# A hybrid encoder step: SSD states handed over with the state index on partitions, final states in 512-column products, scan in runs of four heads

## The chip, the cores and the metric

The kernel runs on one core of one Trainium2 chip. The metric is device microseconds of one execution; lower is better. TensorE (PE in the profile) multiplies matrices, VectorE (DVE), ScalarE (ACT) and GpSimd (POOL) work element by element, and SyncE (SP) issues most of the transfers between memory and the on-chip buffers. An fp32 product that the program writes as one matmul appears as two instructions on PE in the trace.

## The reference

One layer of an encoder works on two groups of tokens that share the weights: 256 tokens of a new stream (the prompt) and the next 32 tokens of a running stream (the sample). Of it, the part that matters here is the SSD mixer: 32 heads of 64 channels in two groups of 16, each head with a state of 64 x 128 numbers. `xs` holds the convolved inputs, `dt` the step sizes, `B` and `C` the projections shared by a group's heads, `a = dt * A` the log decays, and `h0` the old state (zero for the prompt):

```
states = einsum('bclgn,bcgjl,bclgjp->bcgjpn', Bc, decay_states, xc)   # xc = xs * dt
h_last, h_prev = scan: h -> chunk_decay * h + states                  # starts from h0
y = diag part (C B^T, masked and decayed, times xc) + (C h_prev exp(acum)) + D * xs
```

The layer goes on with the gate and a grouped norm, multiplies the concatenation of pooling mixer and SSD mixer with `w_out` (3072 x 2048), adds the input after a norm, and ends in a convolved FFN (2048 -> 2 x 5632 -> 2048). Outputs are the tokens and all new states, among them `h_last` of the prompt and of the sample (32 x 64 x 128 each).

## The kernel before, in words

Activations lie transposed: channels on partitions, 288 tokens (256 + 32) on the free axis. Each weight matrix goes through `project` (L172): blocks of 8 x 128 rows by 256 columns (1 MB) are fetched by SP, split into a high part `whi` on ScalarE (L151) and a low part `wlo` on VectorE (L152), and each 128 x 128 block is multiplied three times (L168 to L170) with the split activations: 288 columns per instruction. The buffers for raw, high and low parts are four deep. Nearly all of TensorE's work is this.

In what order each engine runs its instructions is decided at build time by a scheduler from the program's order, its own estimate of durations, and priorities (a fetch and a split of weights may go ahead); at run time each engine works through its list in that order and waits for what isn't ready. Products land in eight PSUM banks, five for `project` and the state products, three (`aux`) for all else.

The stages around the change:

- B, C and dt columns of `w_in` come first. From dt, `g` holds the running sums of decays of each head over 416 columns (256 for the first 128 source tokens, 128 for the next, 32 for the sample), written to memory as `g_d`. `tok` and `tokd` hold, per token on partitions, the sums, dt, and dt times the decay to the end (`dec`), transposed by TensorE in blocks of 128, 128 and 32 tokens (L464 to L471). `cbt` holds the masked products of B and C (L492 to L501), the sample's as a 32 x 32 block.
- The x columns of `w_in` follow in eight projections of two 128-channel tiles. Each tile is convolved (`conv_out`, L389) and written token by token to memory as `xs_d`.
- The scan of two heads (one 128-channel tile) is `ssd_pair` (L527). `XS_RATE` and `Z_RATE` say after which of the eight x and eight z projections how many pairs are recorded. For every four heads `ssd_four` (L510) loads `g_d` broadcast to all partitions (`gb`) and the old state `h0`, and transposes the state with two products on TensorE (L518) and a ScalarE copy (L520). A pair loads its `xs_d` columns (`xk`), weighs them by dt (`xw`, L540, in two instructions for 128 and 32 rows), makes the decay tables `m` with six Relus (L549), one exponential (L552) and a product with `cbt` (L553), and then multiplies: two prompt blocks (L559, L561), the sample block on 32 rows (L563) and the old state (L565), each for two heads, which sit on the two halves of TensorE's columns. L566 adds D times xs and gives the tile.
- After the scan: gating and norm sums, the u columns of `w_in` with the pooling mixer (`pool_tile`, `pool_group`, L720 to L753), then `w_out` in seven groups of columns (L848). A state step sits between these groups: `state_in` (L805) loads a tile's `xs_d` columns and old state through POOL's queue, and VectorE weighs them (L816 to L819). `state_mm` (L822) multiplies them with B: three products of 128 columns with `xw` stationary and B moving, for two prompt blocks and the sample (32 rows). ScalarE copies the two results out (L832), POOL adds the decayed old state (L833), and SP stores both (L834, L835). Twelve tiles are done three at a time behind four groups; four are kept for the moment when the norm behind `w_out` is computed: one before and three behind `spread` (L585), which sends the norm's factors to all partitions (L864 to L868).
- Then VectorE and ScalarE make the FFN's input tiles `hn` one by one (L872 to L893), and the FFN projections start on them.

Of the kernel before, what the change touches and what calls it, by code (L numbers as in the profile page):

```python
# [11 lines left out]
ALU = mybir.AluOpType  # L12
# [26 lines left out]
XS_RATE = (0, 1, 1, 1, 1, 1, 1, 1)  # L39
Z_RATE = (1, 1, 1, 2, 1, 2, 1, 2)  # L40
# [3 lines left out]
def body(  # L44
# [417 lines left out]
    pool.memset(tok[:, 2, :, :], 0.0)  # L462
    tokd = const.tile([P, 3, HEADS], F32, name="tokd")
    for b, (o, n) in enumerate(BLK):  # L464
        go = (0, 256, 384)[b]
        p_ = aux([P, 3, HEADS], "ptok")
        pe.transpose(p_[:n, 0, :], g[:, go : go + n], id32)
        pe.transpose(p_[:n, 1, :], dt[:, o : o + n], id32)
        pe.transpose(p_[:n, 2, :], dec[:, o : o + n], id32)
        dve.tensor_copy(tok[:n, b, :, :], p_[:n, 0:2, :])  # L470
        dve.tensor_copy(tokd[:n, b, :], p_[:n, 2, :])  # L471

    hv = htile("hv", 2 * NX)
    elast = htile("elast", 1)
    act.activation(elast, g[:, 415:416], AF.Exp)
    dve.tensor_scalar(hv[:, 0:NX], pick, hp[:, 2:3], None, op0=ALU.mult)
    dve.tensor_scalar(hv[:, NX:], pick, elast, None, op0=ALU.mult)
    p_ = aux([P, 2 * NX], "phv")
    pe.matmul(p_, sel64.rearrange("h r q -> h (r q)"), hv, start=True, stop=True)
    dcol = const.tile([P, 2 * NX], F32, name="dcol")  # L480
# [11 lines left out]
    for gi in range(2):  # L492
        blocks_out(b_d, gi, bc[gi], mp)
        p_ = aux([P, MW], "pcb")
        pe.matmul(p_[:, 0:256], bc[gi][:, 0:P], bc[2 + gi][:, 0:NP_], start=True, stop=True)
        pe.matmul(p_[:, 256:384], bc[gi][:, P:NP_], bc[2 + gi][:, P:NP_], start=True, stop=True)
        pe.matmul(p_[:NS, 384:], bc[gi][:, NP_:], bc[2 + gi][:, NP_:], start=True, stop=True)
# [3 lines left out]
        dve.tensor_tensor(cbt[:NS, gi, 384:], p_[:NS, 384:], tri[:NS, :NS], op=ALU.mult)  # L501


    h0v = state_ssd.rearrange("o b (t r) q n -> (r q) (o b t) n", r=2)
    hpv = new_ssd_p.rearrange("o b (t r) q n -> (r q) (o b t) n", r=2)
    hsv = new_ssd_s.rearrange("o b (t r) q n -> (r q) (o b t) n", r=2)
    xs = []
    four = {}

    def ssd_four(q):  # L510

        gb = mp.tile([P, 4, MW], F32, tag="gb", bufs=2, name="gb")
        sp.dma_start(out=gb, in_=g_d[4 * q : 4 * q + 4, :].unsqueeze(0).broadcast_to([P, 4, MW]))
        h0 = mp.tile([P, 2, P], F32, tag="h0", bufs=2, name="h0")
        sp.dma_start(out=h0, in_=h0v[:, 2 * q : 2 * q + 2, :])
        p_ = aux([P, 2, P], "ph0")
        for i in range(2):
            pe.transpose(p_[:, i, :], h0[:, i, :], ident)  # L518
        h0t = mp.tile([P, 2, P], F32, tag="h0t", bufs=2, name="h0t")
# [5 lines left out]
        return gb, h0t, ce  # L525

    def ssd_pair(t):  # L527
        gi = t // 8
        q = t // 2
        if t % 2 == 0:  # L530
            four[q] = ssd_four(q)
        gb, h0t, ce = four[q]
        p_ = mp.tile([P, 3, P], F32, tag="xk", bufs=1, name="xk")
        c = slice(t * P, (t + 1) * P)
        sp.dma_start(out=p_[:, 0:2, :], in_=xs_d[:NP_, c].rearrange("(b p) c -> p b c", p=P))
        sp.dma_start(out=p_[:NS, 2, :], in_=xs_d[NP_:, c])
        xw = mp.tile([P, 3, P], F32, tag="xw", bufs=2, name="xw")
        for b, n in ((slice(0, 2), P), (slice(2, 3), NS)):
            w = tok[:n, b, 1, 2 * t : 2 * t + 2].unsqueeze(3).broadcast_to([n, b.stop - b.start, 2, 64])
            dve.tensor_tensor(  # L540
                xw[:n, b, :].rearrange("p b (r q) -> p b r q", r=2),
                p_[:n, b, :].rearrange("p b (r q) -> p b r q", r=2), w, op=ALU.mult,
            )
        y = aux([P, NT], "py")
        m = mp.tile([P, 2, MW], F32, tag="m", bufs=2, name="m")
        for j in range(2):
            h = 2 * t + j
            for b, (lo_, hi_) in enumerate(((0, 256), (256, 384), (384, MW))):
                act.activation(  # L549
                    m[:, j, lo_:hi_], gb[:, h % 4, lo_:hi_], AF.Relu, bias=tok[:, b, 0, h : h + 1], scale=-1.0  # L550
                )
        act.activation(m, m, AF.Exp, scale=-1.0)  # L552
        dve.tensor_tensor(m, m, cbt[:, gi : gi + 1, :].broadcast_to([P, 2, MW]), op=ALU.mult)  # L553

        for k in range(4):
            for j in range(2):
                c = slice(64 * j, 64 * j + 64)
                if k == 0:
                    pe.matmul(y[c, 0:256], xw[:, 0, c], m[:, j, 0:256], start=True, stop=False)  # L559
                elif k == 1:  # L560
                    pe.matmul(y[c, 128:256], xw[:, 1, c], m[:, j, 256:384], start=False, stop=True)  # L561
                elif k == 2:
                    pe.matmul(y[c, 256:], xw[:NS, 2, c], m[:NS, j, 384:], start=True, stop=False)  # L563
                else:
                    pe.matmul(y[c, 256:], h0t[:, t % 2, c], ce[:, (2 * t + j) % 4, :], start=False, stop=True)  # L565
        dve.scalar_tensor_tensor(xs[t], xs[t], dcol[:, t : t + 1], y, op0=ALU.mult, op1=ALU.add)  # L566
# [80 lines left out]
    pairs = list(range(NX))  # L647
# [4 lines left out]
    def run_pairs(n):  # L652
        for _ in range(n):
            if pairs and pairs[0] < len(xs):
                done[0] = pairs.pop(0)
                ssd_pair(done[0])
# [5 lines left out]
    for i in range(1, NX // 2):  # L662
# [3 lines left out]
        run_pairs(XS_RATE[i])  # L666
    for i in range(NX // 2):
# [5 lines left out]
        run_pairs(Z_RATE[i])  # L673
# [9 lines left out]
    run_pairs(NX)  # L683
    run_gates()
    assert not gates and not pairs
# [15 lines left out]
    op_ = outp.enter_context(tc.tile_pool(name="outp", bufs=1))  # L701
    ubuf = []
    for i in range(4):
        e = op_.tile([P, 350], F32, name=f"ubuf{i}")
# [15 lines left out]
    def pool_tile(i):  # L720
# [6 lines left out]
        while k < w:  # L727
            s = op_.tile([P, 318], F32, tag="win", bufs=3, name="win")
# [5 lines left out]
        d = op_.tile([P, NT], F32, tag="dpool", bufs=2, name="dpool")  # L734
        dve.scalar_tensor_tensor(d[:, :NP_], cur[:, 15:271], 1.0 / w, u[:, 15:271], op0=ALU.mult, op1=ALU.subtract)
        dve.scalar_tensor_tensor(d[:, NP_:], cur[:, 286:318], 1.0 / w, u[:, 286:318], op0=ALU.mult, op1=ALU.subtract)
        a = op_.tile([P, 2, NT], F32R, tag="du", bufs=4, name="du")
# [5 lines left out]
    def pool_group(i):  # L743
        raw = fetch_w(wpv, 2 * i, 2, 0, 256)
        wq = split_w(raw, 0, 2, 256)[0]
        for j in range(2):
# [4 lines left out]
            a = op_.tile([P, 2, NT], F32R, name=f"mixp{2 * i + j}")  # L751
# [23 lines left out]
    xT = op_.tile([P, KD, NT], F32, name="xT2")  # L775
    x1 = []
    msum = op_.tile([P, NT + 32], F32, name="msum")[:, :NT]
# [4 lines left out]
    def mix_out(p_):  # L782
# [4 lines left out]
        else:  # L787
            q = op_.tile([P, NT], F32, name=f"msq{m}")
# [10 lines left out]
    btok = op_.tile([P, 2, 3, P], F32, name="btok")  # L799
    for gi in range(2):  # L800
        c = slice(gi * P, (gi + 1) * P)
        sp.dma_start(out=btok[:, gi, 0:2, :], in_=b_d[:NP_, c].rearrange("(b p) c -> p b c", p=P))
        sp.dma_start(out=btok[:NS, gi, 2, :], in_=b_d[NP_:, c])

    def state_in(t):  # L805

        a = op_.tile([P, 2, NT], F32R, tag="du", bufs=4, name="xw")
        a = a.rearrange("p r c -> p (r c)").bitcast(F32)
        xp, xq, h = a[:, : 2 * P], a[:NS, 2 * P : 3 * P], a[:, 3 * P : 4 * P]
        c = slice(t * P, (t + 1) * P)  # L810
        w = tokd[:, :, 2 * t : 2 * t + 2]
        pool.dma_start(out=xp.rearrange("p (b c) -> p b c", b=2), in_=xs_d[:NP_, c].rearrange("(b p) c -> p b c", p=P))
        pool.dma_start(out=xq, in_=xs_d[NP_:, c])
        pool.dma_start(out=h, in_=h0v[:, t, :])
        o = xp.rearrange("p (b r q) -> p b r q", b=2, r=2)
        dve.tensor_tensor(o, o, w[:, 0:2, :].unsqueeze(3).broadcast_to([P, 2, 2, 64]), op=ALU.mult)  # L816
        o = xq.rearrange("p (r q) -> p r q", r=2)
        dve.tensor_tensor(o, o, w[:NS, 2, :].unsqueeze(2).broadcast_to([NS, 2, 64]), op=ALU.mult)
        dve.tensor_scalar(h, h, dcol[:, NX + t : NX + t + 1], None, op0=ALU.mult)  # L819
        return xp, xq, h  # L820

    def state_mm(t, xp, xq, h, pin=False):  # L822
        gi = t // 8
        st = acc_ps.tile([P, 2, P], F32, tag="acc", name="pst")
        for o, x_, w, i in (
            (0, xp[:, :P], btok[:, gi, 0, :], 0), (0, xp[:, P:], btok[:, gi, 1, :], 1), (1, xq, btok[:NS, gi, 2, :], 2)
        ):
            ins = pe.matmul(st[:, o, :], x_, w, start=i != 1, stop=i != 0)  # L828
            if pin:
                tc.keep_in_program_order(ins)  # L830
        ho = op_.tile([P, 318], F32, tag="win", bufs=3, name="ho")[:, : 2 * P].rearrange("p (r c) -> p r c", r=2)
        act.activation(ho, st, AF.Copy)  # L832
        pool.tensor_tensor(ho[:, 1, :], ho[:, 1, :], h, op=ALU.add)  # L833
        sp.dma_start(out=hpv[:, t, :], in_=ho[:, 0, :])  # L834
        sp.dma_start(out=hsv[:, t, :], in_=ho[:, 1, :])  # L835

    LATE = NX - 4
# [10 lines left out]
    for grp in ((0, 1), (2,), (3,), (4,), (5,), (6,), (7,)):  # L848
# [4 lines left out]
        if grp[0] < 6:  # L853
# [258 lines left out]
```

## Time and profile before

| | |
|---|---|
| median of 3 runs | 1369.47 us (1368.85 to 1371.81) |
| the profiled execution's own time | 1368.83 us |
| its span in the trace | 1367.1 us |
| mean granted TensorE clock | 0.995 |
| scan products in the trace | 116.99 to 269.2 us |
| state products in the trace | 397.2 to 511.4 us |

The span runs from the first to the last instruction in the trace. Rows of a timeline give the start and length in microseconds, the engine, the line of the kernel, the operation with the tiles it writes and reads, its shape on TensorE's array as rows\*columns, the operand's shape, and how many like instructions the row holds. The lengths of matmuls are modelled and overlap, so the distance between starts says what one cost. PEld are the weight loads that run beside the matmuls.

### The profile page before, as it was taken

To read this page: it belongs to the slowest core of one execution; us is meant where nothing else is said; L and a number is where in the kernel's file an instruction comes from. 1 tells how busy PE (TensorE), PEld (TensorE's weight loads), DVE (VectorE), ACT (ScalarE), POOL (GpSimd) and SP (SyncE) were. 2 spreads that over 40 slices of the span, in tenths; PEclk is the share of its full clock that TensorE was granted. 3 is DMA by queue.
4 is the path that set the end of the run, shared out by engine and by line. 5 is a ranking of instruction groups with operands and counts; after the bars stand their busy time and mean duration, and the time that the engine had idled before them with its cause. 6 is when DMAs were issued, how large, how long until landed. Compare 5 with 4: busy or idle time off the path is not lost.

```text
span 1367.1 us, 25869 instructions
## 1 busy us (share of the span) xinstructions
PE 1346.4 (98%) x10247; PEld 1323.9 (97%) x10247; DVE 877.5 (64%) x1551; ACT 670.6 (49%) x1013; POOL 248.7 (18%) x394
## 2 busy tenths in 40 slices
PE   8999999999999999999999999999999999999996
PEld 7999999999999998999999999999999999999995
DVE  5899877669644448877667653334766766764443
ACT  6547766546444345654444443334444444454442
POOL 3233221122233410211112110000211211201110
PEclk9999999999999999999999999999999999999998
DMA  8778875465666634766545455555555545476662
GB/s 267 245 208 254 238 217 188 136 204 176 213 187 185 199 102 148 220 176 196 185 155 172 161 170 170 166 168 168 173 167 167 172 156 183 156 231 187 196 178 91
DMA packets 293287, 250.55 MB, mean 183 GB/s; under 512 B 67344, under 2 KB 286458, under 8 KB 293038
## 3 DMA queue, kind: packets, MB, share of 16 engines
q1 hardware_dynamic: 289962, 242.41, 57.2%
q0 software_dynamic: 2320, 3.86, 0.9%
q10 hardware_dynamic: 884, 2.63, 0.5%
q8 instruction: 80, 1.31, 0.4%
q14 instruction: 41, 0.34, 0.1%
HBM read 234.55 MB, written 14.31 MB: 182 GB/s over the span
## 4 chain that ended last, share of the span: by engine, by line
PE 97%; DVE 2%; DMA 0%; issue 0%; ACT 0%; SPq 0%; DVEq 0%
PE acc L170 31%; PE acc L168 30%; PE acc L169 30%; PE pst L828 1%; PE py L559 1%; DVE wlo L152 0%; DVE xr L1070 0%; DMA xt<-in_x_prompt 0%; DVE hn L880 0%; PE py L563 0%; PE py L565 0%; PE py L561 0%; DVE xsum L892 0%; PE pt L294 0%; DVE mg L875 0%
## 5 line engine op out<-in xcount | busy, mean ns | idle before, releaser
L152 DVE TENSOR_TENSOR wlo<-raw,whi 128x1024 fp32r<-128x1024 f32 (+1 forms) x414 | 494.1, 1194 | 349.5 <-ACT whi L151 348.0
L151 ACT ACTIVATE whi<-raw 128x1024 fp32r<-128x1024 f32 (+1 forms) x414 | 427.7, 1034 | 522.0 <-PE acc L169 423.3
L170 PE MATMUL acc<-hn,wlo 128*128 128x288 f32 x1392 | 413.0, 298 | 1.0 <-DVE wlo L152 1.0
L168 PE MATMUL acc<-hn,whi 128*128 128x288 f32 x1392 | 403.8, 293 | 2.3 <-ACT whi L151 2.2
L169 PE MATMUL acc<-hn,whi 128*128 128x288 f32 x1392 | 403.0, 290 | 0.0
L168 PEld LDWEIGHTS acc<-hn,whi 128*128 128x128 f32 x1392 | 260.0, 188 | 3.5 <-ACT whi L151 3.4
L170 PEld LDWEIGHTS acc<-hn,wlo 128*128 128x128 f32 x1392 | 261.1, 188 | 2.1 <-DVE wlo L152 1.7
L169 PEld LDWEIGHTS acc<-hn,whi 128*128 128x128 f32 x1392 | 261.3, 188 | 0.2 <-DVE hn L880 0.2
L170 PE MATMUL acc<-fa,wlo 128*128 128x288 f32 x704 | 209.3, 297 | 0.0
L170 PE MATMUL acc<-xn,wlo 128*128 128x288 f32 x704 | 209.3, 299 | 0.0
L168 PE MATMUL acc<-xn,whi 128*128 128x288 f32 x704 | 208.3, 298 | 0.0
L169 PE MATMUL acc<-xn,whi 128*128 128x288 f32 x704 | 206.8, 295 | 0.0
L168 PE MATMUL acc<-fa,whi 128*128 128x288 f32 x704 | 206.2, 293 | 0.0
L169 PE MATMUL acc<-fa,whi 128*128 128x288 f32 x704 | 204.3, 290 | 0.0
L168 PEld LDWEIGHTS acc<-xn,whi 128*128 128x128 f32 x704 | 132.8, 189 | 0.5
L169 PEld LDWEIGHTS acc<-xn,whi 128*128 128x128 f32 x704 | 132.9, 189 | 0.4
L170 PEld LDWEIGHTS acc<-xn,wlo 128*128 128x128 f32 x704 | 132.5, 189 | 0.5
L168 PEld LDWEIGHTS acc<-fa,whi 128*128 128x128 f32 x704 | 132.2, 188 | 0.0
L169 PEld LDWEIGHTS acc<-fa,whi 128*128 128x128 f32 x704 | 132.2, 188 | 0.0
L170 PEld LDWEIGHTS acc<-fa,wlo 128*128 128x128 f32 x704 | 132.1, 188 | 0.0
L913 POOL COPY fc_stage<-ebuf 128x4 f32<-128x4 f32 x88 | 28.0, 319 | 506.0 <-DVE ebuf L912 506.0
L919 DVE SCALAR_TENSOR_TENSOR fc<-ebuf,pf,fc 128x290 f32<-128x290 f32 x176 | 90.5, 516 | 3.4 <-ACT fc L917 0.6
(308 smaller groups left out, 1624.6 us busy)
## 6 DMA issues: line engine op xcount, KB each, us to landing
raw<-in_w_up SPq DMA_DIRECT2D x82, 1024.0 KB, 4.9
raw<-in_w_in SPq DMA_DIRECT2D x40, 1024.0 KB, 5.2
raw<-in_w_down SPq DMA_DIRECT2D x32, 1024.0 KB, 5.1
raw<-in_w_out SPq DMA_DIRECT2D x24, 1024.0 KB, 5.4
raw<-in_w_down SPq DMA_DIRECT2D x16, 768.0 KB, 4.6
gb<-g_d SPq DMA_DIRECT2D x8, 832.0 KB, 4.8
raw<-in_w_up SPq DMA_DIRECT2D x12, 512.0 KB, 3.5
raw<-in_w_in SPq DMA_DIRECT2D x6, 512.0 KB, 5.8
```

Of the source, the lines that this page charges most:

```text
L151: act.activation(hi, raw[:, k : k + n, :], AF.Copy)
L152: dve.tensor_tensor(lo, raw[:, k : k + n, :], hi.bitcast(F32), op=ALU.subtract)
L168: pe.matmul(out, wh, a[:, 0, :], start=start, stop=False)
L169: pe.matmul(out, wh, a[:, 1, :], start=False, stop=False)
L170: pe.matmul(out, wl, a[:, 0, :], start=False, stop=stop)
L559: pe.matmul(y[c, 0:256], xw[:, 0, c], m[:, j, 0:256], start=True, stop=False)
L828: ins = pe.matmul(st[:, o, :], x_, w, start=i != 1, stop=i != 0)
L913: pool.tensor_copy(fc_stage[:, :, :, i], e[:, 256:324].rearrange("p (s c) -> p s c", c=34)[:, :, 0:2])
L919: dve.scalar_tensor_tensor(c, e[:, r_ : r_ + 290], pf[:, r_, i : i + 1], c, op0=ALU.mult, op1=ALU.add)
```

## The change

The host hands the old state over as a matrix of 128 state indices by 2048 channels, and takes both new states in that form; it transposes them outside of the device program. In the program:

- `ssd_four` does the whole scan of four heads. Its state tile `h0t` is loaded as it is needed, with no transposes and no copy. `xs_d` goes straight into `xw`, weighed in place by one VectorE instruction of 128 x 768. One exponential and one product with `cbt` serve four heads (128 x 1664). The products go by kind over four heads, in two PSUM banks.
- The sample block is handled on 128 rows: tokens 160 to 287, where only the last 32 rows of `tok`, `tokd` and `cbt` count (the rest is zero in `cbt` and `tokd`).
- The decay of the old state to the end (`elast`) is computed from `gb` on all partitions, four columns per four heads.
- A final state is a product with B stationary and 512 columns of weighed `xs` moving: two for the prompt, one for the sample, for each of four quarters. ScalarE copies the prompt's result out, VectorE adds the decayed old state to the sample's. Three quarters sit behind groups 2, 3 and 4 of `w_out`; of the fourth, the sample's product stands before `spread` and the prompt's two behind it.
- The pooling mixer's buffers get a pool of their own, which is closed when the first state step takes its memory; other tiles are allocated earlier.

The diff, cut to its core:

```diff
-XS_RATE = (0, 1, 1, 1, 1, 1, 1, 1)
-Z_RATE = (1, 1, 1, 2, 1, 2, 1, 2)
+XS_RATE = (0, 0, 0, 1, 0, 1, 0, 1)
+Z_RATE = (1, 0, 1, 0, 1, 1, 1, 0)
...
-        pe.matmul(p_[:NS, 384:], bc[gi][:, NP_:], bc[2 + gi][:, NP_:], start=True, stop=True)
+        pe.matmul(p_[:, 384:], bc[gi][:, NT - P :], bc[2 + gi][:, NP_:], start=True, stop=True)
...
     def ssd_four(q):
...
-        for i in range(2):
-            pe.transpose(p_[:, i, :], h0[:, i, :], ident)
-        act.activation(h0t, p_, AF.Copy)
+        sp.dma_start(out=h0t, in_=state_ssd[:, c])
+        xw = mp.tile([P, 3, 2 * P], F32, tag="xw", bufs=2, name="xw")
+        sp.dma_start(out=xw[:, 0:2, :], in_=xs_d[:NP_, c].rearrange("(b p) c -> p b c", p=P))
+        sp.dma_start(out=xw[:, 2, :], in_=xs_d[NT - P :, c])
...
+        act.activation(elast[:, 4 * q : 4 * q + 4], gb[:, :, MW - 1], AF.Exp)
...
+        dve.tensor_tensor(x4, x4, w, op=ALU.mult)
...
-        dve.tensor_tensor(m, m, cbt[:, gi : gi + 1, :].broadcast_to([P, 2, MW]), op=ALU.mult)
+        dve.tensor_tensor(m, m, cbt[:, gi : gi + 1, :].broadcast_to([P, 4, MW]), op=ALU.mult)
+        ys = [aux([P, NT], "py") for _ in range(2)]
         for k in range(4):
-            for j in range(2):
+            for j in range(4):
...
-                    pe.matmul(y[c, 256:], xw[:NS, 2, c], m[:NS, j, 384:], start=True, stop=False)
+                    pe.matmul(y[:, 256:], xw[:, 2, c], m[:, j, 384:], start=True, stop=False)
...
+    def state_in(j):
...
+        pool.dma_start(out=x[:, 0:2, :], in_=xs_d[:NP_, c].rearrange("(b p) c -> p b c", p=P))
+        pool.dma_start(out=x[:, 2, :], in_=xs_d[NT - P :, c])
+        pool.dma_start(out=h, in_=state_ssd[:, c])
...
+        dve.tensor_tensor(x4, x4, w, op=ALU.mult)
+        dve.tensor_tensor(h3, h3, elast[:, 8 * j : 8 * j + 8].unsqueeze(2).broadcast_to([P, 8, 64]), op=ALU.mult)
...
+    def state_p(j, x, h, pin=False):
+        st = acc_ps.tile([P, 512], F32, tag="acc", name="pst")
+        for b in range(2):
+            ins = pe.matmul(st, btok[:, j // 2, b, :], x[:, b, :], start=b == 0, stop=b == 1)
...
+        act.activation(ho, st, AF.Copy)
+        sp.dma_start(out=new_ssd_p[:, 512 * j : 512 * j + 512], in_=ho)
+    def state_s(j, x, h, pin=False):
...
+        ins = pe.matmul(st, btok[:, j // 2, 2, :], x[:, 2, :], start=True, stop=True)
...
+        dve.tensor_tensor(h, h, st, op=ALU.add)
+        sp.dma_start(out=new_ssd_s[:, 512 * j : 512 * j + 512], in_=h)
...
-    state_mm(LATE, *late_in[0], pin=True)
+    state_s(3, *late_in, pin=True)
     rm = spread(rm_t, "rm", pin=True)
-    for t in range(LATE + 1, NX):
-        state_mm(t, *late_in[t - LATE], pin=True)
+    state_p(3, *late_in, pin=True)
```

More of the change, by code (lines that the diff above doesn't have):

```diff
@@ L461, in body @@
     tok = mp.tile([P, 3, 2, HEADS], F32, name="tok")
-    pool.memset(tok[:, 2, :, :], 0.0)
     tokd = const.tile([P, 3, HEADS], F32, name="tokd")
-    for b, (o, n) in enumerate(BLK):
-        go = (0, 256, 384)[b]
+    pool.memset(tokd[:, 2, :], 0.0)
+    for b, (go, o) in enumerate(((0, 0), (256, P), (288, NT - P))):
         p_ = aux([P, 3, HEADS], "ptok")
[L467 to L478, printed above, removed]
+        pe.transpose(p_[:, 0, :], g[:, go : go + P], id32)
+        pe.transpose(p_[:, 1, :], dt[:, o : o + P], id32)
+        pe.transpose(p_[:, 2, :], dec[:, o : o + P], id32)
+        dve.tensor_copy(tok[:, b, :, :], p_[:, 0:2, :])
+        r_ = slice(P - NS, P) if b == 2 else slice(0, P)
+        dve.tensor_copy(tokd[r_, b, :], p_[r_, 2, :])
+    hv = htile("hv", NX)
+    dve.tensor_scalar(hv, pick, hp[:, 2:3], None, op0=ALU.mult)
+    p_ = aux([P, NX], "phv")
     pe.matmul(p_, sel64.rearrange("h r q -> h (r q)"), hv, start=True, stop=True)
-    dcol = const.tile([P, 2 * NX], F32, name="dcol")
+    dcol = const.tile([P, NX], F32, name="dcol")
     dve.tensor_copy(dcol, p_)
@@ L500, in body @@
         dve.tensor_tensor(cbt[:, gi, 256:384], p_[:, 256:384], tri, op=ALU.mult)
[L501 to L506, printed above, removed]
+        dve.tensor_tensor(cbt[P - NS :, gi, 384:], p_[P - NS :, 384:], tri[P - NS :, P - NS :], op=ALU.mult)
     xs = []
-    four = {}
+    elast = const.tile([P, HEADS + 48], F32, name="elast")
@@ L523, in ssd_four @@
         cs = bc[2 + q // 4][:, NP_:]
         dve.tensor_tensor(ce, ce, cs.unsqueeze(1).broadcast_to([P, 4, NS]), op=ALU.mult)
[L525 to L545, printed above, removed]
-        for j in range(2):
-            h = 2 * t + j
+        w = tok[:, :, 1, 4 * q : 4 * q + 4].unsqueeze(3).broadcast_to([P, 3, 4, 64])
@@ L564, in ssd_pair @@
                 else:
-                    pe.matmul(y[c, 256:], h0t[:, t % 2, c], ce[:, (2 * t + j) % 4, :], start=False, stop=True)
-        dve.scalar_tensor_tensor(xs[t], xs[t], dcol[:, t : t + 1], y, op0=ALU.mult, op1=ALU.add)
+                    pe.matmul(y[:, 256:], h0t[:, c], ce[:, j, :], start=False, stop=True)
+        for i in range(2):
+            t = 2 * q + i
+            dve.scalar_tensor_tensor(xs[t], xs[t], dcol[:, t : t + 1], ys[i], op0=ALU.mult, op1=ALU.add)
     def token_sums(p_, sq, first_, last_, pin=False):
@@ L646, in body @@
     xs_evac(0, xs_ps[0])
-    pairs = list(range(NX))
+    fours = list(range(NX // 2))
     gates = list(range(NX))
@@ L650, in body, with run_fours @@
     rg = []
-    def run_pairs(n):
+    def run_fours(n):
         for _ in range(n):
-            if pairs and pairs[0] < len(xs):
-                done[0] = pairs.pop(0)
-                ssd_pair(done[0])
+            if fours and 2 * fours[0] + 1 < len(xs):
+                q = fours.pop(0)
+                ssd_four(q)
+                done[0] = 2 * q + 1
     def run_gates():
@@ L682, in body @@
                 dve.tensor_tensor(xs[t], xs[t], rg[0], op=ALU.mult)
-    run_pairs(NX)
+    run_fours(NX)
     run_gates()
-    assert not gates and not pairs
+    assert not gates and not fours
     def state_out(stage, n, outs, pool_):
@@ L701, in body @@
     op_ = outp.enter_context(tc.tile_pool(name="outp", bufs=1))
+    mixp = {}
+    for i in (6, 7, 4, 5, 2, 3, 0, 1):
+        mixp[i] = op_.tile([P, 2, NT], F32R, name=f"mixp{i}")
+    xT = op_.tile([P, KD, NT], F32, name="xT2")
+    msum = op_.tile([P, NT], F32, name="msum")
+    btok = op_.tile([P, 2, 3, P], F32, name="btok")
+    msq = [op_.tile([P, NT], F32, name=f"msq{m}") for m in range(2)]
+    xsum = op_.tile([P, NT], F32, name="xsum")
+    poolp = ExitStack()
+    up_ = poolp.enter_context(tc.tile_pool(name="poolp", bufs=1))
     ubuf = []
     for i in range(4):
-        e = op_.tile([P, 350], F32, name=f"ubuf{i}")
+        e = up_.tile([P, 350], F32, name=f"ubuf{i}")
         pool.memset(e, 0.0)
@@ L802, in body @@
         sp.dma_start(out=btok[:, gi, 0:2, :], in_=b_d[:NP_, c].rearrange("(b p) c -> p b c", p=P))
[L803 to L828, printed above, removed]
+        sp.dma_start(out=btok[:, gi, 2, :], in_=b_d[NT - P :, c])
+    stp = []
+    def state_in(j):
+        if not stp:
+            poolp.close()
+            stp.append(outp.enter_context(tc.tile_pool(name="stp", bufs=1)))
+        x = stp[0].tile([P, 3, 512], F32, tag="sx", bufs=2, name="sx")
+        h = stp[0].tile([P, 512], F32, tag="sh", bufs=2, name="sh")
+        c = slice(512 * j, 512 * j + 512)
+        pool.dma_start(out=x[:, 0:2, :], in_=xs_d[:NP_, c].rearrange("(b p) c -> p b c", p=P))
+        pool.dma_start(out=x[:, 2, :], in_=xs_d[NT - P :, c])
+        pool.dma_start(out=h, in_=state_ssd[:, c])
+        x4 = x.rearrange("p b (r q) -> p b r q", r=8)
+        w = tokd[:, :, 8 * j : 8 * j + 8].unsqueeze(3).broadcast_to([P, 3, 8, 64])
+        dve.tensor_tensor(x4, x4, w, op=ALU.mult)
+        h3 = h.rearrange("p (r q) -> p r q", r=8)
+        dve.tensor_tensor(h3, h3, elast[:, 8 * j : 8 * j + 8].unsqueeze(2).broadcast_to([P, 8, 64]), op=ALU.mult)
+        return x, h
@@ L852, in body @@
         )
-        if grp[0] < 6:
-            for t in range(LATE * (grp[0] - 2) // 4, LATE * (grp[0] - 1) // 4) if grp[0] else ():
-                state_mm(t, *state_in(t))
+        if 2 <= grp[0] < 5:
+            x_h = state_in(grp[0] - 2)
+            state_p(grp[0] - 2, *x_h)
+            state_s(grp[0] - 2, *x_h)
         elif grp[0] == 6:
-            late_in = [state_in(t) for t in range(LATE, NX)]
+            late_in = state_in(3)
         if grp[0] == 0:
@@ L1110 @@
     r = _run(nc, [arrays], core_ids=[0])
-    return tuple(r.results[0][f"out_{i}"] for i in range(len(_OUTS)))
+    outs = [_np.asarray(r.results[0][f"out_{i}"]) for i in range(len(_OUTS))]
+    for i in (6, 7):
+        outs[i] = _np.ascontiguousarray(outs[i].T).reshape(1, 1, HEADS, 64, P)
+    return tuple(outs)
```

53 lines of the change are left out of this document (27 added, 26 removed).

## The prediction

> **What bounds the kernel now.** I read first the page's busy line and its chain of work that ended last.
>
> ```profile
> PE 1346.4 (98%) x10247; PEld 1323.9 (97%) x10247; DVE 877.5 (64%) x1551; ACT 670.6 (49%) x1013; POOL 248.7 (18%) x394
> PE 97%; DVE 2%; DMA 0%; issue 0%; ACT 0%; SPq 0%; DVEq 0%
> ```
>
> The first line is busy time and share of the span; the second the chain's shares. TensorE is on the chain for 97% of the span. What it need not do shortens the run wherever nothing else is late behind it. Next I read the stretches that hold the edited code: the scan, the output projection with the final states, and the step to the FFN.
>
> ```profile
> 100.00:200.00 100.00, 100.00 (x795) 93.09 (x794) 89.05 (x197) 71.80 (x149) 29.54 (x24) 1.00 0.83 242
> 400.00:500.00 100.00, 100.00 (x744) 97.70 (x745) 42.39 (x64) 39.20 (x54) 35.45 (x57) 1.00 0.55 170
> 506.40:544.00 37.60, 35.23 (x242) 32.10 (x241) 33.33 (x71) 22.05 (x45) 2.52 (x4) 1.00 0.42 127
> ```
>
> After the length come PE, PEld, DVE, ACT and POOL busy, then the granted clock (1.00). In the first two TensorE has no gap. In the third it idles 2.4 us while VectorE is busy 33.3 of 37.6: there VectorE is the limit.
>
> So the question is what the scan and the state products cost on TensorE beyond their columns. One pair of heads in the timeline, then three rows of narrower looks at the same stretch:
>
> ```profile
> 121.55 0.29 PE L170 MATMUL acc<-xn,wlo 128*128 128x288 f32 x1
> 121.68 0.29 PE L168 MATMUL acc<-xn,whi 128*128 128x288 f32 x1
> 121.90 0.65 PE L559 MATMUL py<-m,xw 128*64 128x256 f32 x4
> 122.38 0.39 PE L561 MATMUL py<-m,xw 128*64 128x128 f32 x4
> 122.70 0.30 PE L563 MATMUL py<-m,xw 32*64 32x32 f32 x4
> 122.94 0.31 PE L565 MATMUL py<-ce,h0t 128*64 128x32 f32 x4
> 123.17 0.40 PE L169 MATMUL acc<-xn,whi 128*128 128x288 f32 x1
> 123.41 0.29 PE L170 MATMUL acc<-xn,wlo 128*128 128x288 f32 x1
> ```
>
> ```profile
> 122.17 0.39 PE L559 MATMUL py<-m,xw 128*64 128x256 f32 x2
> 122.49 0.28 PE L561 MATMUL py<-m,xw 128*64 128x128 f32 x2
> 122.78 0.22 PE L563 MATMUL py<-m,xw 32*64 32x32 f32 x2
> ```
>
> Look at starts: ends are modelled and overlap. A projection matmul follows the last after 0.13 us. An fp32 product is two instructions, and the two heads' column halves run together. A half step takes 0.21 us for 256 columns (122.17 to 122.38), 0.11 for 128 (122.38 to 122.49), 0.08 for 32 (122.70 to 122.78). One pair's eight half steps are thus 2 x 0.21 + 2 x 0.11 + 4 x 0.08 = 0.96 us. All else appears where the shape on the array (128\*128, 128\*64, 32\*64) changes: entering 0.09 (121.68 to 121.90 against 0.13) and 0.06 in the step behind it; leaving 0.07 in the last step and 0.11 in the first projection matmul (0.24 against 0.13): **0.33 a run**. Going to 32 rows costs 0.10 (122.49 to 122.70 against 0.11), coming back 0.08 (122.78 to 122.94).
>
> **The change, part by part.**
>
> *The scan.* In the timeline the fp32 work of the scan stands in 22 runs; here are the first and the last:
>
> ```profile
> 116.99 0.38 PE L518 MATMUL ph<-ident,h 128*128 128x128 f32 x2
> 267.90 0.65 PE L559 MATMUL py<-m,xw 128*64 128x256 f32 x4
> ```
>
> 21 of them hold scan products, since 565 often follows some matmuls after 563. Eight have a pair of transposes of the old state, each such pair 0.20 us:
>
> ```profile
> 128.34 0.44 PE L518 MATMUL ph<-ident,h 128*128 128x128 f32 x2
> 128.54 0.38 PE L170 MATMUL acc<-xn,wlo 128*128 128x288 f32 x1
> ```
>
> The scan now costs 16 x 0.96 = 15.4, 21 x 0.33 = 6.9, 8 x 0.20 = 1.6, and 16 x 0.10 + 9 x 0.08 = 2.3 of row changes (seven pairs are parted at the second): 26.2 us. The changed program has the same 64 products in 9 runs (eight of four heads, one of them parted), no transposes, and the sample block on 128 rows, so that no row change is left inside a run: 15.4 + 9 x 0.33 = 18.4. **Saved: 7.8 us.**
>
> The row change is the doubtful term: no row shows a scan run without one. It is bounded by 0 (it stays) and 2.3 (it goes). I take that it goes, by the state products, where both kinds stand side by side:
>
> ```profile
> 397.09 0.29 PE L170 MATMUL acc<-mixp,wlo 128*128 128x288 f32 x1
> 397.23 3.13 PE L828 MATMUL pst<-btok,xw 128*128 128x128 f32 x18
> 400.28 0.40 PE L168 MATMUL acc<-mixs,whi 128*128 128x288 f32 x1
> 400.52 0.29 PE L169 MATMUL acc<-mixs,whi 128*128 128x288 f32 x1
> ```
>
> ```profile
> 397.33 0.50 PE L828 MATMUL pst<-btok,xw 128*128 128x128 f32 x3
> 397.76 0.37 PE L828 MATMUL pst<-btok,xw 32*128 32x128 f32 x1
> 397.97 0.58 PE L828 MATMUL pst<-btok,xw 32*128 32x128 f32 x2
> ```
>
> The four halves on 128 rows start at 397.23, 397.33, 397.45 and 397.56 (three of 0.28 in 0.50 us stand 0.11 apart), though the stationary operand changes among them; before, between and behind the two on 32 rows the steps are 0.20, 0.21 and 0.20. A new operand alone is free, a new shape is not.
>
> [...]
>
> *Final states.* Four bursts like this cost 3.05 us plus 0.11 for leaving: 12.6. The changed program has three bursts of three 512-column products ahead of the FFN step, all on 128\*128. By 0.11 for 128 and 0.21 for 256 columns a half of 512 takes 0.43, a product 0.86: 3 x 3 x 0.86 = 7.7. **Saved: 4.9 us.** No row shows 512 fp32 columns. The bounds: 0.86, and four times the present 3.05 / 9 = 0.34, 1.36, which leaves 0.4 of the saving. I take 0.86, by the 256-column rows, the nearest.
>
> *The late products.* Behind the last projection there is one group ahead of the spread and three behind it:
>
> ```profile
> 506.45 1.10 PE L828 MATMUL pst<-btok,xw 128*128 128x128 f32 x6
> 507.48 0.85 PE L589 MATMUL rm<-ident,rm 128*128 128x128 f32 x6
> 508.17 3.21 PE L828 MATMUL pst<-btok,xw 128*128 128x128 f32 x18
> 511.32 0.67 PE L168 MATMUL acc<-hn,whi 128*128 128x288 f32 x3
> ```
>
> The first becomes one product: 0.86 for 1.03. The state add, now 512 columns on VectorE, stands ahead of the first x1 multiply (508.38 in the trace, behind the spread). By m's 832 columns in 1.05 us (below) it takes about 0.7; it can start when the product is out, near 507.5, and ends by 508.2, so it costs nothing; if it is late, some tenths. The three behind become 1.7 us for 3.1, but VectorE sets the pace until 544: I count 0, at best 1.4.
>
> *B and C products.* The two of 32 columns become 128\*128:
>
> ```profile
> 113.10 0.70 PE L495 MATMUL pcb<-bc 128*128 128x256 f32 x2
> 113.64 0.38 PE L496 MATMUL pcb<-bc 128*128 128x128 f32 x2
> 113.95 0.25 PE L497 MATMUL pcb<-bc 128*32 128x32 f32 x2
> 114.13 0.70 PE L495 MATMUL pcb<-bc 128*128 128x256 f32 x2
> ```
>
> 1.03 us a group against some 0.75 without shape changes: **saved 0.5** in two.
>
> *VectorE, ScalarE, transfers.* At nothing, covered by TensorE:
>
> ```profile
> L553 DVE TENSOR_TENSOR m<-m,cbt 128x832 f32<-128x832 f32 x16 | 16.8, 1049 | 3.6 <-ACT m L552 3.6
> L552 ACT ACTIVATE m<-m 128x832 f32<-128x832 f32 x16 | 14.2, 888 | 0.1
> L549 ACT ACTIVATE m<-gb,tok x96: 304/388/513, 111.0 to 255.4; 128x256 f32<-128x256 f32 x32, 128x128 f32<-128x128 f32 x32, 128x32 f32<-128x32 f32 x32
> ```
>
> ```profile
> DVE xw L816 <- DMA xw<-xs_d: 12.5, 4, 5.7
> raw<-in_w_out SPq DMA_DIRECT2D x24, 1024.0 KB, 5.4
> ```
>
> (Counts, mean ns; then the waits: total, times, longest us; then a weight fetch: KB, us to landing.) Doubled tiles (m 128x1664, about 2.0 us, its exponential 1.7, by twice the rows) add few elements, and fixed parts go; ScalarE loses eight copies and gains eight tiny exponentials.
>
> A new wait: each state group loads 1 MB through POOL's queue, and VectorE's 128x1536 product (some 1.9 us by m's row) waits for it, the weight splits (wlo) queued behind, TensorE behind those. Today VectorE waited up to 5.7 us there without a gap on TensorE. The first load takes over buffers of the pooling mixer and waits for its last product; in the new order 297 matmuls (39 us by 0.13) lie between that and the first state product. The loads of the third and fourth group wait for product and store two groups back, and POOL's sums of squares (msum) stand behind them; those are wanted only at 505. 1 MB of weights lands in 5.4 us, so I let a group's load take 5 to 10, hidden. On SP a four's loads wait for TensorE's products two fours back, with weight fetches behind; four raw buffers of 48 matmuls each (6.3 us) are the cover, and each us beyond it would show whole. SP issues 8 state stores for 32 and 16 scan loads for 32, so fetches pass fewer.
>
> Sum: 7.8 + 4.9 + 0.5 = 13.2. Against the profiled run's own 1368.83: 1355.6. The median of the runs is 0.64 above that run; I forecast **1356.2 us**.
>
> **Rivals.**
> *Uncovered loads.* The row-change price stays in the scan (2.3) and each of nine state products pays 0.1 (0.9): 1359.4. For it: the extra is a constant 0.1. Against: the 0.11 steps above.
> *Dear wide products.* 1.36 each: 4.5 come back, 1360.7. Against: 0.11 and 0.21 are in proportion.
> *The four comes late* (ends slower). A burst needs twelve Relus (4.7), an exponential of 1.7 and a VectorE product of 2.0, some 8.4 us in one chain, against half for a pair. VectorE is 89% busy there; two bursts stand only 29 matmuls (3.8 us) apart. Where tables aren't made a four ahead, TensorE waits up to 4.6. Once: 1360.8. It turns slower only if all eight wait over 2 us: 8 x 2.2 = 17.6, 1373.8. Against: two buffers of m and gb, and most bursts stand 12 us and more apart in the new order.
> *The state loads land late.* Beyond the 5.7 us that are hidden today, each of three groups would add its excess; with 3 us each, 1365.
> *The late products count*: 1354.8.
>
> **How the numbers follow.** Forecast 0.55, late products 0.06, uncovered loads 0.09, wide products 0.06, one late four or some late loads 0.11, within 0.2% (several of these together) 0.05, slower (eight late fours) 0.08. The range 1353.5 to 1364 leaves out the last two, some late loads and a little below. 0.2% (2.7 us) is about what a measurement of this kernel can tell: faster 0.87, same 0.05, slower 0.08.
>
> **What would show it.** Scan runs of about 2.25 us (2 x 0.96 + 0.33) in nine places, with 0.11 between the 128- and 32-column steps; state products of 0.86; the stretch behind the spread as long as now; no gap on TensorE from 100 to 500. Wrong if TensorE idles ahead of a scan run or a state product, or if wlo comes late there.

## The result, and the profile after

The changed kernel takes 1354.12 us (median of 4 runs, 1352.97 to 1354.60) against 1369.82 us (median of 4 runs, the three above and one more): a ratio of 0.9882, 95% interval 0.9865 to 0.9899, or 15.7 us. The forecast was 1356.2, with a gain of 13.2 us on the profiled run. The profiled run of the changed kernel takes 1352.97 us, so 15.9 came off there; its span is 1351.1 us for 1367.1.

The busy line and the chain of work that ended last, from the page after:

```profile
PE 1330.3 (98%) x10159; PEld 1311.0 (97%) x10159; DVE 873.0 (65%) x1482; ACT 664.4 (49%) x992; POOL 210.1 (16%) x342
...
PE 96%; DVE 2%; DMA 1%; issue 0%; ACT 0%; DVEq 0%
```

TensorE is still the bound, and its busy time fell by 16.1 us, as much as the span: work went away, and no new wait took its place. The same three stretches as before (length, then PE, PEld, DVE, ACT and POOL busy, granted clock, DMA share, GB/s), the third from the sums of squares to the FFN step:

```profile
100.00:200.00 100.00, 100.00 (x820) 96.43 (x820) 91.44 (x177) 74.75 (x153) 20.24 (x25) 1.00 0.90 265
400.00:500.00 100.00, 100.00 (x721) 95.01 (x719) 44.91 (x51) 41.39 (x59) 11.89 (x11) 1.00 0.51 165
490.07:527.27 37.20, 34.86 (x230) 30.64 (x229) 33.21 (x72) 21.45 (x43) 0.00 (x0) 1.00 0.41 128
```

TensorE has no gap in the first two. VectorE is busier in the scan (91.4 of 100), yet nothing waits for it there. In the third VectorE is the limit as before; GpSimd's 2.5 us have gone from it.

A run of four heads in the timeline of the changed kernel:

```profile
126.24 0.29 PE L169 MATMUL acc<-xn,whi 128*128 128x288 f32 x1
126.46 1.08 PE L538 MATMUL py<-m,xw 128*64 128x256 f32 x8
127.37 0.61 PE L540 MATMUL py<-m,xw 128*64 128x128 f32 x8
127.81 0.38 PE L542 MATMUL py<-m,xw 128*64 128x32 f32 x8
128.01 0.41 PE L544 MATMUL py<-ce,h0t 128*64 128x32 f32 x8
128.34 0.40 PE L170 MATMUL acc<-xn,wlo 128*128 128x288 f32 x1
128.58 0.29 PE L168 MATMUL acc<-xn,whi 128*128 128x288 f32 x1
```

Read the starts again. Entering takes 0.22 against 0.13, leaving 0.24 against 0.13: 0.09 and 0.11, as before. Between them lie 1.89 us, so the run costs 2.09. From the first 32-column row to the second (127.81 to 128.01) four half steps take 0.20 us, 0.05 each. All nine runs of the trace are entered in 0.09 or 0.10, so no run waited for its tables. The scan's runs add up to 17.2 us, where those of the kernel before add up to 26.1.

A burst of final states and the step to the FFN:

```profile
387.26 1.88 PE L817 MATMUL pst<-sx,btok 128*128 128x512 f32 x4
388.98 1.02 PE L826 MATMUL psts<-sx,btok 128*128 128x512 f32 x2
...
389.97 0.29 PE L169 MATMUL acc<-mixs,whi 128*128 128x288 f32 x1
...
491.43 1.10 PE L826 MATMUL psts<-sx,btok 128*128 128x512 f32 x2
...
492.96 1.96 PE L817 MATMUL pst<-sx,btok 128*128 128x512 f32 x4
494.74 0.80 PE L168 MATMUL acc<-hn,whi 128*128 128x288 f32 x4
```

Two prompt products take 1.72 us (387.26 to 388.98), 0.86 each; a burst takes 2.58 with the one projection matmul that 389.97 follows taken off.

**Where 16.0 us came from.** At the first edited instruction, a small transpose of `g`, the changed kernel is 0.59 us ahead (101.06 us against 101.65), by nothing that was edited: TensorE's clock rose sooner. Two projection matmuls at nearly the same time, before and after:

```profile
11.28 0.44 PE L170 MATMUL acc<-xn,wlo 128*128 128x288 f32 x1
11.52 0.44 PE L169 MATMUL acc<-xn,whi 128*128 128x288 f32 x1
```

```profile
10.78 0.29 PE L170 MATMUL acc<-xn,wlo 128*128 128x288 f32 x1
10.91 0.29 PE L169 MATMUL acc<-xn,whi 128*128 128x288 f32 x1
```

They stand 0.24 us apart in the kernel before and 0.13 after. The record of the granted clock begins with full clock at 12.58 us before and at 10.25 us after. In the ten profiles of this study it does so between 10.25 and 13.70 us, and the transpose stands between 100.88 and 102.36 us, latest where the clock rose last. At the first late state product (506.45 and 491.43) it is 15.0 ahead, at the end of the span 16.0. So 14.4 us come from the scan and the output projection: 26.1 - 17.2 = 8.9 in the scan's runs, 12.7 - 7.7 = 5.0 in the early states, 0.3 in the B and C products, and 0.2 that is left over in scattered steps; and 1.0 comes after the last projection, where nothing was expected.

### The profile page after: what moved, and what is told of

It reads as the page before. It is cut to its first block, busy times and chain, and to the rows that moved or that the text cites. A ratio compares the mean times of both kernels' runs of the same rounds, so it can differ in the third digit from the quotient of the medians.

```text
span 1351.1 us, 25380 instructions
## 1 busy us (share of the span) xinstructions
PE 1330.3 (98%) x10159; PEld 1311.0 (97%) x10159; DVE 873.0 (65%) x1482; ACT 664.4 (49%) x992; POOL 210.1 (16%) x342
## 4 chain that ended last, share of the span: by engine, by line
PE 96%; DVE 2%; DMA 1%; issue 0%; ACT 0%; DVEq 0%
PE acc L170 31%; PE acc L168 30%; PE acc L169 30%; PE py L538 1%; DMA raw<-in_w_in 1%; DVE wlo L152 1%; PE pst L817 1%; DVE xr L1063 0%; DVE hn L873 0%; PE py L540 0%; PE psts L826 0%; DVE xsum L885 0%; DMA xt<-in_x_prompt 0%; DVE mg L868 0%; DVE mg L867 0%
## 6 DMA issues: line engine op xcount, KB each, us to landing
raw<-in_w_up SPq DMA_DIRECT2D x12, 512.0 KB, 3.5
raw<-in_w_in SPq DMA_DIRECT2D x6, 512.0 KB, 5.3
```

## Experiments

**The sample block back on 32 rows.** Line 542 of the changed kernel alone:

```diff
-pe.matmul(y[:, 256:], xw[:, 2, c], m[:, j, 384:], start=True, stop=False)
+pe.matmul(y[:, 256:], xw[P - NS :, 2, c], m[P - NS :, j, 384:], start=True, stop=False)
```

> The changed kernel, but the scan's sample product (line 542) takes its stationary and moving operand from the last 32 rows only (the other 96 rows of its table are zero), so that two changes of rows come back into every run; all else is the same, instruction for instruction. Drain theory (a change of the shape on the array costs, a new operand doesn't): each of the nine runs gets longer by 0.10 going to 32 rows and 0.08 to 0.10 coming back, eight complete runs of 2.09 us become some 2.3, in all 1.5 to 2 us (2.6 if the 32-column steps also grow from 0.05 to 0.08): 1355.5 to 1356.7 us. Uncovered-load theory (the constant 0.1 is a load that is not hidden, whatever its rows): the runs stay at 2.09 us and the time at 1354.1.

Measured: 1356.10 us (1355.59 to 1356.73), ratio to the kernel before 0.9908 (0.9893 to 0.9922). The same four groups in its timeline:

```profile
127.83 0.61 PE L540 MATMUL py<-m,xw 128*64 128x128 f32 x8
128.36 0.42 PE L542 MATMUL py<-m,xw 32*64 32x32 f32 x8
128.71 0.42 PE L544 MATMUL py<-ce,h0t 128*64 128x32 f32 x8
129.07 0.40 PE L170 MATMUL acc<-xn,wlo 128*128 128x288 f32 x1
```

The steps are 0.53, 0.35 and 0.36 us, for 0.44, 0.20 and 0.33 on 128 rows: 0.27 more for each group of four heads (0.09 going, 0.15 within the group on 32 rows and coming back, 0.03 behind). One of the eight groups holds its two pairs one behind the other and pays twice; in all it is 2.4 us. The operands' number and order are unchanged. Uncovered loads would have left the runs as they were, so that rival falls here.

**Runs of two heads.** The second pair of a four is issued at the next slot:

```diff
-        ys = [aux([P, NT], "py") for _ in range(2)]
-        for k in range(4):
-            for j in range(4):
+        ssd_pair(q, 0, xw, m, h0t, ce)
+        half.append((q, 1, xw, m, h0t, ce))
...
     def run_fours(n):
+        if half:
+            ssd_pair(*half.pop())
```

> The changed kernel with the products of a four issued as two pairs, the second pair at the next slot; tables, loads and the sample block on 128 rows stay. The products stand in 12 runs, eight of them of a single pair, in place of 9. If a run costs by its entering and leaving (0.09 + 0.11 in the traces, up to 0.33 as priced in the prediction), the three runs more cost 0.6 to 1.0 us: 1354.7 to 1355.1. By the prediction's steps a pair alone on 128 rows takes 0.96 + 0.33 = 1.29 us where the kernel before shows 1.47 with its changes of rows; if 32-column steps are 0.05, as two of the changed kernel's groups suggest, it takes about 1.15. If instead the changed kernel gained by issuing more instructions of one kind in a row (no price per run, but a price per step in short runs), the pair stays near 1.47 less 0.2 and the total grows by over 1.5 us.

Measured: 1355.53 us (1353.89 to 1355.82), ratio 0.9901 (0.9886 to 0.9916). A pair that stands alone:

```profile
132.66 0.29 PE L168 MATMUL acc<-xn,whi 128*128 128x288 f32 x1
132.89 0.65 PE L544 MATMUL py<-m,xw 128*64 128x256 f32 x4
133.37 0.39 PE L546 MATMUL py<-m,xw 128*64 128x128 f32 x4
133.59 0.26 PE L548 MATMUL py<-m,xw 128*64 128x32 f32 x4
133.68 0.29 PE L550 MATMUL py<-ce,h0t 128*64 128x32 f32 x4
133.89 0.40 PE L169 MATMUL acc<-xn,whi 128*128 128x288 f32 x1
134.13 0.30 PE L170 MATMUL acc<-xn,wlo 128*128 128x288 f32 x1
```

It costs 0.09 + 1.00 + 0.11 = 1.20 us; the kernel before takes 1.47 for the same columns, so the 0.27 of the experiment above is the whole difference, and no price per step in short runs is left over. Two such runs cost 2.40 against 2.09 for a four: a run costs 0.31, close to the 0.33 of the prediction. The 12 runs add up to 17.9 us, 0.7 above the nine, as expected. The profiled run's span is 2.7 us longer than the changed kernel's: beside the 0.7, its clock rose later at the start (0.5), and TensorE lost 1.4 us at 524 to 528, in code that was not touched (last section). What share these have in the median was not measured.

**State products of 128 columns, on 128 and on 32 rows.** The three early bursts of the changed kernel cut into 128 columns, prompt and sample in turn; in the first kernel r is all 128 rows, in the second the last 32:

```diff
+        for o in range(0, 512, P):
+            c = slice(o, o + P)
+            for b in range(2):
+                pe.matmul(st[:, c], btok[:, j // 2, b, :], x[:, b, c], start=b == 0, stop=b == 1)
+            pe.matmul(ss[:, c], btok[r, j // 2, 2, :], x[r, 2, c], start=True, stop=True)
```

> The changed kernel with the three early bursts of final states cut into 128 columns, prompt, prompt, sample for each 128 columns in turn, all on 128 rows; the same columns are streamed, with 24 instructions a burst for 6. Rows theory: the saving of the final states is that of the changes of rows, the width of 512 is worth nothing; a burst takes 12 x 2 x 0.11 = 2.6 us as now: 1354.1. Width theory: 512 columns are needed to hide the loads of the stationary operand; a burst takes 3.06 x 12 / 9 = 4.1 us, and the time is 3 x 1.5 = 4.5 us longer, 1358.6.

> As the kernel with 128-column state products in turn, but the sample products take their operands from the last 32 rows only: four times to 32 rows and back in each of three bursts (the last return falls on the projection behind). Rows theory: a burst grows from 2.6 by 4 x (0.10 + 0.20) less the 0.11 of leaving at the end, to 3.7 to 4.1 us; the time is 3.5 to 4.5 us above that of its 128-row sister, near 1358. Width theory: no more than its sister. Uncovered loads: no more than its sister.

Measured: 1354.11 us (1353.37 to 1356.02) on 128 rows, ratio 0.9898 (0.9881 to 0.9914), and 1358.55 (1357.86 to 1359.50) on 32, ratio 0.9926 (0.9911 to 0.9941). The beginning of a burst, on 128 rows and on 32:

```profile
387.38 0.61 PE L839 MATMUL pst<-sx,btok 128*128 128x128 f32 x4
387.82 0.39 PE L840 MATMUL psts<-sx,btok 128*128 128x128 f32 x2
388.04 0.61 PE L839 MATMUL pst<-sx,btok 128*128 128x128 f32 x4
```

```profile
388.56 0.61 PE L839 MATMUL pst<-sx,btok 128*128 128x128 f32 x4
389.10 0.48 PE L840 MATMUL psts<-sx,btok 32*128 32x128 f32 x2
389.51 0.71 PE L839 MATMUL pst<-sx,btok 128*128 128x128 f32 x4
```

A group of three products takes 0.66 us on 128 rows (387.38 to 388.04), six halves of 0.11, though each product has another stationary operand. With the sample product on 32 rows it takes 0.95 the first time (388.56 to 389.51) and 1.06 from then on. A burst is 2.7 us in the first kernel (2.6 for 512 columns), 4.2 in the second. So the width is worth 0.1 a burst and the rows 1.5: the final states' saving is that of the sample block on 128 rows. With leaving counted, the three bursts on 32 rows cost 12.7 us (3 x 4.23), as much as the four of the kernel before (4 x 3.17), which stream as many columns with the two operands exchanged: the exchange by itself is worth nothing. By these kernels a change to 32 rows and back costs 0.27 us in the scan and 0.39 on average in the bursts.

**More work behind the spread.** The last quarter's prompt products are issued twice:

```diff
-        for b in range(2):
+        for i in range(4 if pin else 2):
+            b = i % 2
```

> The changed kernel with the two prompt products of the last quarter behind the spread issued twice (the second time over the first): 1.76 us more work for TensorE at the place where the prediction counts its time at nothing. VectorE theory (VectorE's chain from the spread to the FFN sets the pace; TensorE waits some 6 us for it later on): the time stays within 0.2 us of the changed kernel's, and TensorE's waits in that stretch shrink by 1.7 us. TensorE theory (the late products count): 1.8 us longer, near 1355.9.

Measured: 1354.30 us (1353.58 to 1354.68), ratio 0.9891 (0.9874 to 0.9907): the interval is too wide to tell 1.8 us, so the trace has to. The doubled products push the first FFN matmul back by 1.3 us, and the 1.3 are made up before VectorE's chain ends. The profiled run lost 1.4 us just behind that, to the clock (last section), and with those taken off its span is the changed kernel's within 0.2. VectorE sets the pace there.

**The last state add on GpSimd.**

```diff
-        dve.tensor_tensor(h, h, st, op=ALU.add)
+            act.activation(ho, st, AF.Copy)
+            pool.tensor_tensor(h, h, ho, op=ALU.add)
```

> The changed kernel with the last quarter's state add put back on GpSimd (ScalarE copies the product out, GpSimd adds), as before the change. Contention theory: the changed kernel's stretch behind the spread got 0.76 us shorter because no GpSimd add runs beside VectorE's row multiplies any more; with it back those multiplies take 0.5 to 0.7 us for 0.45 again while it lasts, VectorE's chain grows from 32.5 to about 33.2 us, and the time by 0.6 to 0.8, to 1354.8. Rival (the chain got shorter because the prompt products behind the spread did, so TensorE's part counts): the chain stays at 32.5 us, and the time too.

Measured: 1353.70 us (1353.07 to 1355.99), ratio 0.9890 (0.9875 to 0.9905); so small a step can't be told from the times. In the trace it can. GpSimd's add and the VectorE instructions beside and behind it in this experiment:

```profile
493.06 1.27 POOL L832 TENSOR_TENSOR sh<-sh,ho 128x512 f32<-128x512 f32 x1 [19.67 <-ACT ho L831]
```

```profile
493.47 1.18 DVE L873 TENSOR_TENSOR mg<-mg,xT 128x288 f32<-128x288 f32 x1
...
495.04 0.46 DVE L873 TENSOR_TENSOR mg<-mg,xT 128x288 f32<-128x288 f32 x1
```

The same instruction takes 1.18 us while GpSimd adds and 0.46 afterwards, and VectorE's chain from its first multiply to its last sum grows by 0.7 us, from 32.5 to 33.2. In the kernel before, three of the four adds of the late groups did the same. By the starts of VectorE's instructions the first, at 508.10, cost it nothing, the second some 0.2 us and the last two 0.48, of 0.76 in all; here are the last two, VectorE beside them, and the same two VectorE instructions after the change:

```profile
511.80 1.53 POOL L833 TENSOR_TENSOR ho<-ho,xw 128x128 f32<-128x128 f32 x2 [1.31 <-ACT ho L832]
```

```profile
512.29 0.72 DVE L875 TENSOR_TENSOR mg<-mg,xT 128x288 f32<-128x288 f32 x1
512.93 0.71 DVE L880 SCALAR_TENSOR_TENSOR hn<-mg,pb,hn 128x288 fp32r<-128x288 f32 x1
```

```profile
496.82 0.45 DVE L868 TENSOR_TENSOR mg<-mg,xT 128x288 f32<-128x288 f32 x1
497.19 0.51 DVE L873 SCALAR_TENSOR_TENSOR hn<-mg,pb,hn 128x288 fp32r<-128x288 f32 x1
```

**Prompt products moved behind the spread.** What costs nothing there can be moved there: the third quarter's prompt products,

```diff
-            state_p(grp[0] - 2, *x_h)
+            if grp[0] < 4:
+                state_p(grp[0] - 2, *x_h)
+            else:
+                late_p.append((grp[0] - 2, x_h))
...
     state_p(3, *late_in, pin=True)
+    for j, x_h in late_p:
+        state_p(j, *x_h, pin=True)
```

> The changed kernel with the third quarter's two prompt products moved from their place in the output projection to behind the spread, next to the last quarter's. VectorE theory: 1.72 us leave TensorE's path and hide in its waits behind the spread: 1352.4, ratio to the kernel before 0.987. TensorE theory: no change, 1354.1.

and the second quarter's too (3 in place of 4 in the first added line, and the buffers shared out anew: three for the prompt columns, one for the sample's, one for the old state).

> As the one before, with the second quarter's prompt products moved too (prompt columns and sample columns of the states in buffers of their own, so that three quarters can wait). VectorE theory: 3.4 us leave the path, 1350.7; the extra 3.4 us behind the spread still fit in the 6 us of waits, and it is less only where the early waits are used up before the chain's end, or where VectorE's order around the loads changes. TensorE theory: no change.

Measured: 1351.16 us (1350.94 to 1352.87) for one quarter moved, ratio 0.9871 (0.9857 to 0.9886), and 1350.81 (1349.87 to 1352.85) for two, ratio 0.9868 (0.9853 to 0.9883).

```profile
489.82 1.10 PE L826 MATMUL psts<-sx,btok 128*128 128x512 f32 x2
...
491.35 3.68 PE L817 MATMUL pst<-sx,btok 128*128 128x512 f32 x8
```

With one quarter moved, the late state product starts at 489.82 for 491.43, VectorE's chain takes no longer than it did (32.3 us for 32.5), and the span is 1349.4 for 1351.1: the whole 1.7 us are won, as the VectorE theory said. All four of its runs lie below all four of the two kernels above. With two, 1.7 more are won ahead of the spread, but VectorE's chain gets 1.2 us longer, and TensorE loses 1.4 to the clock behind it in the profiled run. ScalarE then has three copies of 512 columns among those that VectorE's chain takes in; that this is what lengthens it was not tried. The two kernels are not told apart by their times.

## Why the prediction was right, and where its sizes were off

- *TensorE is the bound, and what it sheds shortens the run:* right; busy time and span fell by the same 16 us.
- *Scan, 7.8 us:* 8.9. The mechanism was right in each part: the row changes go (first experiment), a run costs 0.31 for the 0.33 forecast (second), entering and leaving are as before. The term that was mis-sized is the 32-column half step. The prediction took 0.08 us for it from a row in which it stood between two changes of rows; on 128 rows it is 0.05 (127.81 to 128.01, four steps). That makes a four 2.09 us, for the 2.25 forecast, and the row change 0.27 there and back, not 0.18. The kernel before came out right all the same (26.2 for 26.1), because what the step had too much the row change had too little.
- *Final states, 4.9 us:* 5.0. The product takes the 0.86 us that was taken from the 128- and 256-column rows, and the dear wide products fall. The reason is in the rows, not in the width: 128 columns would have cost 0.1 a burst more.
- *B and C products, 0.5 us:* 0.3. The first group starts at 112.05 and the second at 112.95,

```profile
112.05 0.70 PE L492 MATMUL pcb<-bc 128*128 128x256 f32 x2
...
112.81 0.31 PE L494 MATMUL pcb<-bc 128*128 128x32 f32 x2
112.95 0.68 PE L492 MATMUL pcb<-bc 128*128 128x256 f32 x2
113.47 0.38 PE L493 MATMUL pcb<-bc 128*128 128x128 f32 x2
```

  0.90 us a group, where 0.75 was forecast without shape changes. No shape changes in these rows, and yet the 32-column product takes 0.14 us (112.81 to 112.95) for twice 0.05 in the scan, and the two halves of 256 columns behind it 0.52 for 0.42. So "a new operand alone is free" holds here beside products of 128 columns and more, and not beside one of 32. The weight loads of these rows start 0.11 us apart where they are closest (two from 112.70, two from 112.92), more than a 32-column step; a load that is not covered would fit that, but it was not tried.
- *The prompt products behind the spread, counted 0:* right. They got 1.4 us shorter without effect, and doubling them has none. The measured 1354.1 lies nearer to the rival that counts them (1354.8) than to the forecast (1356.2), but for another reason (next point).
- *VectorE, ScalarE, GpSimd, transfers at nothing:* right for the waits, wrong in one place. VectorE waited for its loads,

```profile
DVE sh L811 <- DMA sh<-in_state_ssd: 8.0, 2, 4.1
...
DVE sx L809 <- DMA sx<-xs_d: 1.8, 2, 1.3
```

  up to 4.1 us at a time, and TensorE had no gap: the cover held, and neither late fours nor late state loads showed. But the prediction priced the state add only by what it puts on VectorE (0.69 us, hidden as it said) and not by what it takes off GpSimd. The adds had been slowing VectorE in the one stretch where VectorE is the bound; without them its chain is 0.76 us shorter, instruction for instruction the same. With 0.2 in the steps around the spread that is the 1.0 us won after the last projection.
- The rest of the excess, 0.6 us, is the start, where the clock rose at 12.58 us before and at 10.25 after, and between 10.25 and 13.70 in the ten profiles. By the spans the gain over the forecast, 2.8 us, is thus 1.1 in the scan, 1.0 behind the last projection, 0.6 in the start, 0.1 in the states and 0.2 left over, less 0.2 in the B and C products. The 1.0 has a cause that the prediction doesn't have, and the 0.6 is luck.

## What to carry to other kernels

Count changes of the shape on the array before columns: an idle three quarters of the rows, fed with zeros or with tokens whose weights are zero, can be cheaper than a product cut to the rows that it needs (by 0.27 us for four heads here). Take the price of a step from a row without the thing that is to be removed, or the two are mixed up. Where an engine that is not the bound hands work to another, ask also whom it was disturbing (0.76 us of VectorE's chain here); and where one engine sets the pace for a stretch, move the other's work there (1.7 us won with one quarter here), as long as it doesn't lengthen the chain that sets the pace.

## What the runs showed of the hardware

**GpSimd and VectorE.** With the last state add on GpSimd, one VectorE instruction of 288 columns took 1.18 us beside that add of 512 columns, and 0.46 behind it; the add itself took 1.27.

**The clock behind short waits.** In three of the ten profiles TensorE's granted clock was half for 3.41 us near the end of VectorE's chain, and projection matmuls came 0.24 us apart for 0.13, which cost 1.4 us. In the traces' record of the clock, full clock lasts 1341.44 us in the kernel before, 1327.79 in the changed kernel, and 512.0 and 815.8 us, ahead of the fall and behind it, in the kernel with doubled products: 393, 389, 150 and 239 times 3.413 us, the length of the fall. By these lengths, as an estimate, windows of 3.413 us can be laid over each trace from where its full clock begins. Here are the window ahead of the fall and the window of the fall in the kernel with doubled products, and the two at the same place in the kernel with 128-column state products on 128 rows, which kept its clock:

```profile
519.50:522.91 3.41, 2.08 (x13) 1.38 (x11) 3.41 (x8) 3.02 (x6) 0.00 (x0) 1.00 0.04 14
522.91:526.33 3.42, 3.42 (x15) 3.42 (x16) 2.97 (x6) 0.87 (x2) 0.00 (x0) 0.50 0.69 222
```

```profile
519.88:523.29 3.41, 2.29 (x14) 1.59 (x12) 3.41 (x8) 3.29 (x6) 0.00 (x0) 1.00 0.05 17
523.29:526.70 3.41, 3.20 (x22) 3.06 (x23) 3.25 (x7) 0.87 (x2) 0.00 (x0) 1.00 0.63 188
```

The counts include matmuls that were still running as the window began: 10 of the 13 start in the first, 12 of the 14 in the third. Ahead of the three falls, 10, 10 and 11 projection matmuls start in the window (a full one has 26). In all ten profiles no other window from 508 to 545 us that holds no state product has fewer than 12. TensorE's waits are much the same in these kernels, with no two starts more than 1.0 us apart; what differs is where the windows fall on them, and that goes with the loss of the clock. Whether it is the matmuls or the busy time that counts was not measured.

TensorE was not idle ahead of the fall above: it was busy for 2.08 of 3.41 us. For reading times: three of the ten spans here hold 1.4 us of such a fall, seven hold none. Whether the same kernel has it in one execution and not in another was not shown.
